# The low part of q on all 128 partitions: the second score pass of a differential attention at 128 rows

## Chip, cores, metric

One core of a Trainium2 chip runs the whole program. The metric is device time in microseconds of one execution. The engines are TensorE (PE in the profile; its weight loads appear as a lane of their own, PEld), VectorE (DVE), ScalarE (ACT), GpSimd (POOL) and SyncE (SP), which issues most DMAs.

## What is computed

Two layers of a hybrid decoder on a sequence of 512 tokens, width 1024. In each layer one input projection feeds four mixers (an S5 state space, a differential attention, an RG-LRU and a cross-attention into 256 memory tokens), each is gated, and an output projection is added to x. The change lies in the differential attention, of which this is the core of the reference:

```python
s1 = jnp.einsum('bqhd,bkhd->bhqk', qblk[..., 0, :], k1).astype(F32)
s2 = jnp.einsum('bqhd,bkhd->bhqk', qblk[..., 1, :], k2).astype(F32)
s1 = jnp.where(mask, s1, -1e30)
s2 = jnp.where(mask, s2, -1e30)
p = jax.nn.softmax(s1, axis=-1) - lam * jax.nn.softmax(s2, axis=-1)
return jnp.einsum('bhqk,bkhd->bqhd', p.astype(v.dtype), v)
```

There are 4 heads with two 64-wide halves m = 0, 1 each, a causal mask, and query blocks of 128.

## The kernel before

Everything is f32. To use the faster f32r matmuls without losing precision, the kernel splits an operand into a high part (rounded to f32r by a cast) and a low part (what the cast left over), and multiplies high by high, high by low and low by high, accumulating in PSUM. The projections (`cm_block`, matmul line L508, and `tm_block`, matmul line L528) do that with three passes per piece of weight, 128 rows by 256 or 512 columns, and they make up most of TensorE's work. ScalarE casts the weights' high part (`whi`, L166), VectorE subtracts the low part (`wlo`, L172).

Attention (`attention`, L601) runs beside these projections as a generator: after each piece of a projection a tick lets the live generators put in their next step, and the Tile scheduler then fixes the order on each engine and gives out the buffers of the pools. Items are pairs (query block i, head h), 16 per layer. `scores(n)` makes, for m = 0 and 1, a tile of scores of N = 128 (i + 1) columns, but at least 256 are streamed. The keys `kT[m]` hold on the 64 partitions of half m the high part of k and on the other 64 partitions its low part. The queries' high part `qh` stands on both halves of the partitions, so that one pass with 128 rows (L638) gives qh·k_high + qh·k_low. The second pass (L639) multiplies the queries' low part `ql` by k_high: it uses only the 64 partitions of half m, both of the stationary tile and of the keys. A third pass (L640), in bf16, adds the causal mask from an identity and a constant tile. There are 64 of each pass in the program. Then VectorE takes the maximum (L642), ScalarE the exponentials into `e` (L648), VectorE combines both halves (L654); later TensorE transposes (`ptrans`, L662) and multiplies by v (`av`, L672).

`q_parts(i)` is called at the first head of a block: two casts per half on ScalarE (L622, L623) fill both partition halves of `qh`, and one subtraction per half on VectorE (issued in the helper `tt`, L340) fills `ql`. `qh` comes from the pool `mid` (tag b4, four buffers of 4 KB per partition), which also holds `e`, the memory tiles and the normalised x; `ql` comes from `sm2` (tag b2, nine buffers of 2 KB).

Of the kernel before, what the change touches and what calls it, by code (L numbers as in the profile page):

```python
# [10 lines left out]
F32R = mybir.dt.float32r  # L11
# [3 lines left out]
ALU = mybir.AluOpType  # L15
AX = mybir.AxisListType

P = 128
# [72 lines left out]
def tile_kernel(ctx: ExitStack, tc: tile.TileContext, A, out):  # L91
    nc = tc.nc
    V, S, G, PE = nc.vector, nc.scalar, nc.gpsimd, nc.tensor
# [11 lines left out]
    def nm(s):  # L105
        uid[0] += 1
        return f"{s}_{uid[0]}"
# [4 lines left out]
    def b4(shape, name, dtype=F32):  # L112
        return mid.tile(shape, dtype, tag="b4", name=nm(name))

    def b2(shape, name, dtype=F32):
        return sm2.tile(shape, dtype, tag="b2", name=nm(name))

    def ti(n, name):
        return tiny.tile([P, n], F32, tag=name, name=nm(name))
# [4 lines left out]
    def sc2(shape):  # L124
        return ps.tile(list(shape), F32, tag="sc", bufs=1, name=nm("sc"))

    def tp(shape=(P, 4, 128)):
        return ps.tile(list(shape), F32, tag="tp", bufs=2, name=nm("tp"))

    def ms(shape):  # L130
        return ps.tile(list(shape), F32, tag="tp", bufs=2, name=nm("ms"))
# [153 lines left out]
    def norm_h(t):  # L285

        h = b4([P, D], "h")
        r = rstd_of(xs(t), D, h)
        scale_h(h, t, r)
        return h  # L290
# [27 lines left out]
    for t in range(NT):  # L318
        h, hn = hn, (norm_h(t + 1) if t + 1 < NT else None)
# [19 lines left out]
    def tt(o, a, b, op):  # L339
        V.tensor_tensor(out=o, in0=a, in1=b, op=op)  # L340
# [260 lines left out]
    def attention(l, R):  # L601
        while pend or "par" in st.live:
            yield
        qT, kT, v = R["qT"][0], R["kT"], R["v"]
        o = qT
        R["o"] = o
        oss = const.tile([P, 16], F32, tag="oss", name=nm("oss"))
        R["oss"] = oss
        items = [(i, h) for i in range(NT) for h in range(4)]
        n_it = len(items)  # L610
        live = {}

        qs_ = {}

        def q_parts(i):

            qi = qT[:, :, i * 128:(i + 1) * 128]
            qh = b4([P, 2, 4, 128], "qh", F32R)
            ql = b2([P, 4, 128], "ql", F32R)
            for m in range(2):  # L620
                own, oth = slice(m * 64, m * 64 + 64), slice(64 - m * 64, 128 - m * 64)
                S.copy(qh[own, m], qi[own])  # L622
                S.copy(qh[oth, m], qi[own])  # L623
                tt(ql[own], qi[own], qh[own, m], ALU.subtract)
            qs_[i] = (qh, ql)

        def scores(n):
            i, h = items[n]
            N = (i + 1) * 128

            M = max(N, 256)
            s = sc2((P, 2, 512))
            if h == 0:
                q_parts(i)
            qh, ql = qs_[i]
            for m in range(2):
                own = slice(m * 64, m * 64 + 64)
                PE.matmul(s[:, m, :M], qh[:, m, h, :], kT[m][:, h, :M], start=True, stop=False)  # L638
                PE.matmul(s[:, m, :M], ql[own, h, :], kT[m][own, h, :M], start=False, stop=False)  # L639
                PE.matmul(s[:, m, i * 128:N], idb, cmb, start=False, stop=True)  # L640
            mx = ti(2, "mx")
            V.tensor_reduce(out=mx, in_=s[:, :, :N], op=ALU.max, axis=AX.X)  # L642
            nmx = ti(2, "nmx")
            V.tensor_scalar(out=nmx, in0=mx, scalar1=-0.125, scalar2=None, op0=ALU.mult)
            e = b4([P, 2, 512], "e")
            sm = ti(2, "sm")
            for m in range(2):
                S.activation(e[:, m, :N], s[:, m, :N], AF.Exp, bias=nmx[:, m:m + 1], scale=0.125,  # L648
                             accum_out=sm[:, m:m + 1])
            rc = ti(2, "rc")  # L650
            V.reciprocal(rc, sm)
            cc = ti(1, "cc")
            V.tensor_scalar(out=cc, in0=sm[:, 0:1], scalar1=nlam[:, l:l + 1], scalar2=rc[:, 1:2], op0=ALU.mult, op1=ALU.mult)
            V.scalar_tensor_tensor(out=e[:, 0, :N], in0=e[:, 1, :N], scalar=cc, in1=e[:, 0, :N], op0=ALU.mult, op1=ALU.add)  # L654
            live[n] = (e, rc, None)

        def ptrans(n):
            i, h = items[n]
            e, rc, _ = live[n]
            pt = tp()  # L660
            for j in range(i + 1):
                PE.transpose(pt[:, j, :], e[:, 0, j * 128:(j + 1) * 128], ident)  # L662
            pT = b2([P, 4, 128], "pT")
            S.copy(pT[:, :i + 1, :], pt[:, :i + 1, :])
            live[n] = (None, rc, pT)

        def av(n):
            i, h = items[n]
            _, rc, pT = live.pop(n)
            a = ms((P, 128))  # L670
            for j in range(i + 1):
                PE.matmul(a, pT[:, j, :], v[:, j, h * 128:(h + 1) * 128], start=(j == 0), stop=(j == i))  # L672
            S.activation(o[:, h, i * 128:(i + 1) * 128], a, AF.Copy, scale=rc[:, 0:1])
            jk = b2([P, 128], "jk")
            S.activation(jk, a, AF.Square, scale=rc[:, 0:1], accum_out=oss[:, i * 4 + h:i * 4 + h + 1])

        for n in range(n_it + 2):
            if n < n_it:
                scores(n)
            if n >= 2:  # L680
                av(n - 2)
            yield D_AT[0]
            if 1 <= n <= n_it:
                ptrans(n - 1)
                yield D_AT[1]
# [416 lines left out]
    for pi, (l, n, u, ids) in enumerate(plan):  # L1102
# [93 lines left out]
        elif n == "gl":  # L1196
# [4 lines left out]
            for hf, pid in enumerate(ids):  # L1201
                whi, wlo = (w.rearrange("p (k s c) -> p k s c", k=2, s=2) for w in w_use(pid))
                for j in range(2):
                    for s in (1, 0):
                        a = gacc[j][s]
                        i = 0
                        for k in range(2):
                            for w, h in ((whi, yhi), (whi, ylo), (wlo, yhi)):
                                PE.matmul(a, w[:, k, s, j * 128:(j + 1) * 128], h[:, 2 * hf + k, :],  # L1209
                                          start=(hf == 0 and i == 0), stop=(hf == 1 and i == 5))  # L1210
# [112 lines left out]
```

## Time and profile before

| | |
|---|---|
| median of 3 runs | 934.51 us (934.37 to 934.92) |
| profiled execution | 934.99 us |
| its span, first to last instruction | 933.2 us |
| mean granted TensorE clock | 0.997 |
| busy: PE, PEld, DVE, ACT, POOL | 908.3, 751.0, 645.2, 521.4, 42.8 us |

A row of the timeline gives the start of an instruction in us from the start of the span, its length, engine, line and operands. Matmuls are pipelined, so their lengths overlap: what a matmul costs is the distance from its start to the next one's, and the length holds the way through the array as well. The windows give busy time by engine in a stretch; the chain follows the work that ended last back from release to release.

### The profile page before, as it was taken

How to read it: one execution, taken by the hardware profiler on the slowest of the kernel's cores; microseconds unless marked ns; L12 is line 12 of the kernel's file. 1: busy time of each engine (PE TensorE's matmuls, PEld its weight loads, DVE VectorE, ACT ScalarE, POOL GpSimd, SP SyncE). 2: the span in 40 equal slices, each digit the busy share in tenths (PEclk: the TensorE clock that was granted, in tenths of full speed). 3: DMA queues.
4: the chain of work that ended last, by engine and by line, in shares of the span. 5: the costliest groups of instructions: out<-in, count | busy, mean ns of one | idle time of the engine just before them, and what ended most of it. 6: DMA issues, size and time to landing. Idle time of an engine off the chain costs nothing.

```text
span 933.2 us, 12492 instructions
## 1 busy us (share of the span) xinstructions
PE 908.3 (97%) x4538; PEld 751.0 (80%) x4538; DVE 645.2 (69%) x1297; ACT 521.4 (56%) x1038; POOL 42.8 (5%) x94
## 2 busy tenths in 40 slices
PE   6999999999999989999999999999999999999997
PEld 4788878877888878888888888788778888788885
DVE  6975877458999965893373675853698998667343
ACT  6674776987343355831454579665646333764123
POOL 1001000001011100000100000000101110000000
PEclk9999999999999999999999999999999999999999
DMA  5833432103213225532343321421212222243222
GB/s 198 210 103 99 137 91 68 46 23 94 68 50 116 71 69 186 142 113 91 106 162 105 91 91 46 147 89 59 72 48 70 72 72 68 68 155 117 93 88 91
DMA packets 81072, 90.59 MB, mean 97 GB/s; under 512 B 23793, under 2 KB 58226, under 8 KB 81010
## 3 DMA queue, kind: packets, MB, share of 16 engines
q1 hardware_dynamic: 77986, 85.98, 29.8%
q10 hardware_dynamic: 720, 2.62, 0.8%
q0 software_dynamic: 2304, 1.18, 0.5%
q8 instruction: 36, 0.59, 0.3%
q14 instruction: 26, 0.21, 0.1%
HBM read 84.92 MB, written 4.19 MB: 95 GB/s over the span
## 4 chain that ended last, share of the span: by engine, by line
PE 78%; DVE 14%; ACT 4%; DMA 2%; issue 2%; SPq 1%; DVEq 0%; ACTq 0%
PE acc L528 37%; PE acc L508 19%; PE acc L1209 5%; DVE u L340 3%; PE sc L639 2%; DVE wlo L172 2%; PE ms L672 2%; PE tp L1032 1%; PE sc L638 1%; DVE xr L1015 1%; PE sc L640 1%; PE tp L826 1%; PE tp L305 1%; PE tp L662 1%; PE sc L801 1%
## 5 line engine op out<-in xcount | busy, mean ns | idle before, releaser
L166 ACT CAST whi<-raw 128x1024 fp32r<-128x1024 f32 x136 | 143.2, 1053 | 224.4 <-PE acc L528 123.8
L172 DVE TENSOR_TENSOR wlo<-raw,whi 128x1024 fp32r<-128x1024 f32 x136 | 166.1, 1222 | 120.8 <-ACT whi L166 120.3
L508 PE MATMUL acc<-hThi,whi 128*128 128x512 f32 x384 | 155.3, 404 | 0.3 <-DVE bg L709 0.3
L508 PE MATMUL acc<-hThi,wlo 128*128 128x512 f32 x384 | 153.1, 399 | 0.0
L508 PE MATMUL acc<-hTlo,whi 128*128 128x512 f32 x384 | 152.7, 398 | 0.0
L528 PE MATMUL acc<-whi,hThi 128*128 128x512 f32 x256 | 105.1, 410 | 0.8 <-ACT whi L166 0.8
L528 PE MATMUL acc<-wlo,hThi 128*128 128x512 f32 x256 | 101.7, 397 | 0.0
L528 PE MATMUL acc<-whi,hTlo 128*128 128x512 f32 x256 | 101.1, 396 | 0.0
L528 PE MATMUL acc<-whi,mxl 128*128 128x512 f32 x256 | 100.2, 391 | 0.0
L528 PE MATMUL acc<-whi,mxh 128*128 128x512 f32 x256 | 100.2, 391 | 0.0
L528 PE MATMUL acc<-wlo,mxh 128*128 128x512 f32 x256 | 100.2, 391 | 0.0
L508 PEld LDWEIGHTS acc<-hThi,wlo 128*128 128x128 f32 x384 | 72.6, 189 | 14.2
L508 PEld LDWEIGHTS acc<-hThi,whi 128*128 128x128 f32 x384 | 72.7, 189 | 13.5 <-DVE bg L709 0.7
L508 PEld LDWEIGHTS acc<-hTlo,whi 128*128 128x128 f32 x384 | 72.8, 190 | 12.9
L528 PEld LDWEIGHTS acc<-whi,hThi 128*128 128x128 f32 x256 | 56.4, 220 | 8.9 <-ACT whi L166 1.2
L528 PEld LDWEIGHTS acc<-whi,hTlo 128*128 128x128 f32 x256 | 56.3, 220 | 7.7 <-DVE hTlo L308 0.2
L528 PEld LDWEIGHTS acc<-wlo,hThi 128*128 128x128 f32 x256 | 56.6, 221 | 7.1
L528 PEld LDWEIGHTS acc<-whi,mxl 128*128 128x128 f32 x256 | 48.1, 188 | 9.8
L528 PEld LDWEIGHTS acc<-whi,mxh 128*128 128x128 f32 x256 | 48.1, 188 | 9.7
L528 PEld LDWEIGHTS acc<-wlo,mxh 128*128 128x128 f32 x256 | 48.1, 188 | 9.6
L642 DVE TENSOR_REDUCE mx<-sc 128x2 f32<-128x256 f32 (+3 forms) x32 | 26.3, 823 | 36.3 <-PE sc L640 36.2
L966 POOL DMA_DIRECT2D MT<-kq x64 | 32.1, 508 | 376.3 <-DVE kq L340 233.5
(305 smaller groups left out, 1671.5 us busy)
## 6 DMA issues: line engine op xcount, KB each, us to landing
raw<-in_w_in_dram SPq DMA_DIRECT2D x80, 512.0 KB, 3.6
raw<-in_w_out_dram SPq DMA_DIRECT2D x32, 512.0 KB, 3.3
raw<-in_w_mem_kv_dram SPq DMA_DIRECT2D x16, 512.0 KB, 3.3
x<-in_x_dram SPq DMA_DIRECT2D x8, 512.0 KB, 5.2
raw<-in_s_w_glu_dram SPq DMA_DIRECT2D x16, 256.0 KB, 3.1
mt<-in_mem_dram SPq DMA_DIRECT2D x4, 512.0 KB
xd<-x SPq DMA_DIRECT2D x4, 512.0 KB, 4.3
x<-xd SPq DMA_DIRECT2D x4, 512.0 KB, 7.0
```

What stands on the lines that cost most here:

```text
L166: S.copy(hi, wbuf[j])
L172: V.tensor_tensor(out=lo, in0=raw, in1=hi, op=ALU.subtract)
L305: lastins["pe"] = PE.transpose(pt[:, k, :], h[:, kk * 128:(kk + 1) * 128], ident)
L340: V.tensor_tensor(out=o, in0=a, in1=b, op=op)
L508: PE.matmul(a[j][:, :ncol], w[:, kk, c], h(k), start=(hf == 0 and i == 0), stop=(hf == 1 and i == 3 * nh - 1))
L528: PE.matmul(a[t], h(k, t), w[:, kk, :], start=(p == 0 and kk == 0 and i == 0), stop=(p == np_ - 1 and kk == 1 and i == 2))
L638: PE.matmul(s[:, m, :M], qh[:, m, h, :], kT[m][:, h, :M], start=True, stop=False)
L639: PE.matmul(s[:, m, :M], ql[own, h, :], kT[m][own, h, :M], start=False, stop=False)
L642: V.tensor_reduce(out=mx, in_=s[:, :, :N], op=ALU.max, axis=AX.X)
L672: PE.matmul(a, pT[:, j, :], v[:, j, h * 128:(h + 1) * 128], start=(j == 0), stop=(j == i))
L966: G.dma_start(out=MT[g * 64 + 64 - n:g * 64 + 64, g, t], in_=kq[g * 64:g * 64 + n])
L1209: PE.matmul(a, w[:, k, s, j * 128:(j + 1) * 128], h[:, 2 * hf + k, :], start=(hf == 0 and i == 0), stop=(hf == 1 and i == 5))
```

## The change

`ql` gets the shape of `qh`, one copy per half m, from the pool `mid`. For each half the subtraction is made twice, once onto the half's own partitions and once, from the same inputs, onto the other 64. The second pass then takes all 128 rows of `ql` and of `kT[m]`: besides ql·k_high it adds ql·k_low, a term that was left out before.

```diff
             qh = b4([P, 2, 4, 128], "qh", F32R)
-            ql = b2([P, 4, 128], "ql", F32R)
+            ql = b4([P, 2, 4, 128], "ql", F32R)
             for m in range(2):
                 own, oth = slice(m * 64, m * 64 + 64), slice(64 - m * 64, 128 - m * 64)
                 S.copy(qh[own, m], qi[own])
                 S.copy(qh[oth, m], qi[own])
-                tt(ql[own], qi[own], qh[own, m], ALU.subtract)
+                tt(ql[own, m], qi[own], qh[own, m], ALU.subtract)
+                tt(ql[oth, m], qi[own], qh[own, m], ALU.subtract)
...
             for m in range(2):
-                own = slice(m * 64, m * 64 + 64)
                 PE.matmul(s[:, m, :M], qh[:, m, h, :], kT[m][:, h, :M], start=True, stop=False)
-                PE.matmul(s[:, m, :M], ql[own, h, :], kT[m][own, h, :M], start=False, stop=False)
+                PE.matmul(s[:, m, :M], ql[:, m, h, :], kT[m][:, h, :M], start=False, stop=False)
                 PE.matmul(s[:, m, i * 128:N], idb, cmb, start=False, stop=True)
```

The scheduler orders the engines anew. On TensorE, at the first item of layer 0's third query block (`sc` is the tile of scores, `acc` a projection's accumulator), the order before was:

```order
L638 MATMUL sc_1599<-kT_751,qh_1600 128x384
L639 MATMUL sc_1599<-kT_751,ql_1601 128x384
L640 LDWEIGHTS idb
L640 MATMUL sc_1599<-cmb,idb 128x128
L672 MATMUL ms_1627<-v_546,pT_1578 128x128
L638 MATMUL sc_1599<-kT_752,qh_1600 128x384
L672 MATMUL ms_1627<-v_546,pT_1578 128x128
L508 MATMUL acc_1633<-hThi_122,whi_1489 128x512
L639 MATMUL sc_1599<-kT_752,ql_1601 128x384
```

and of the change, from the last of the dense matmuls that now stand between the first and the second pass:

```order
L508 MATMUL acc_1639<-hThi_122,wlo_1495 128x512
L639 MATMUL sc_1603<-kT_751,ql_1605 128x384
L640 LDWEIGHTS idb
L640 MATMUL sc_1603<-cmb,idb 128x128
L638 MATMUL sc_1603<-kT_752,qh_1604 128x384
L662 MATMUL tp_1659<-cst,e_1539 128x128 x2
```

Twelve projection matmuls now stand between the item's first L638 and its L639, and eight between the second L638 and its L639, where there was one.

On VectorE, at the last query block of layer 1 (`rc`, `cc`, `e`: the softmax of the item before; `mx`: the maximum of the new one), the order before was:

```order
L654 SCALAR_TENSOR_TENSOR e_6087<-e_6087,cc_6093 128x384
L340 TENSOR_TENSOR ql_6157<-qT_4578,qh_6156 64x512 x2
L172 TENSOR_TENSOR wlo_6200<-raw_6037,whi_6198 128x1024
L642 TENSOR_REDUCE mx_6170<-sc_6155 128x2
L340 TENSOR_TENSOR qm_6030<-acc_6031,qm_6029 128x512
```

and of the change:

```order
L654 SCALAR_TENSOR_TENSOR e_6101<-e_6101,cc_6107 128x384
L340 TENSOR_TENSOR ql_6171<-qT_4586,qh_6170 64x512 x4
L172 TENSOR_TENSOR wlo_6216<-raw_6051,whi_6214 128x1024
L642 TENSOR_REDUCE mx_6186<-sc_6169 128x2
L340 TENSOR_TENSOR qm_6044<-acc_6045,qm_6043 128x512
```

The place is the same, with four subtractions in it instead of two.

## Rows read from the trace of the kernel before

**Rows 1.** The page, busy time and share of the span by engine.
```profile
PE 908.3 (97%) x4538; PEld 751.0 (80%) x4538; DVE 645.2 (69%) x1297; ACT 521.4 (56%) x1038; POOL 42.8 (5%) x94
```

**Rows 2.** The chain that ended last, shares by line.
```profile
by line: PE acc L528 37.1%; PE acc L508 18.6%; PE acc L1209 4.6%; DVE u L340 3.1%; PE sc L639 2.4%; DVE wlo L172 1.9%; PE ms L672 1.8%; issue 1.5%; PE tp L1032 1.4%; PE sc L638 1.4%; DVE xr L1015 1.4%; PE sc L640 1.1%; PE tp L826 1.1%; PE t
```

**Rows 3.** Windows: stretch, its length, busy PE, PEld, DVE, ACT, POOL, PEclk, DMA.
```profile
85.00:210.00 125.00, 124.88 (x638) 101.39 (x637) 82.28 (x159) 96.87 (x212) 3.93 (x10) 1.00 0.24 74
577.00:693.00 116.00, 116.00 (x603) 94.67 (x601) 77.81 (x152) 68.42 (x167) 4.04 (x8) 1.00 0.26 78
655.00:700.00 45.00, 45.00 (x231) 34.63 (x230) 37.12 (x73) 22.99 (x54) 4.04 (x8) 1.00 0.18 53
700.00:800.00 100.00, 98.70 (x551) 84.26 (x550) 88.32 (x161) 47.60 (x107) 12.00 (x24) 1.00 0.23 71
```

**Rows 4.** Waits of the weight loads: who waited for whom, total us, times, longest.
```profile
PEld sc L639 <- issue: 10.0, 38, 0.4
...
PEld L640 <- issue: 6.6, 31, 0.2
...
PEld sc L639 <- DVE ql L340: 0.4, 1, 0.4
```

**Rows 5.** Timeline of the weight loads around one item of 256 columns.
```profile
101.94 0.19 PEld L638 LDWEIGHTS sc<-kT,qh 128*128 128x128 f32 x1
102.26 0.18 PEld L639 LDWEIGHTS sc<-kT,ql 64*128 64x128 f32 x1
102.57 0.10 PEld L640 LDWEIGHTS <-idb 128*128 128x128 bf16 x1
102.58 0.20 PEld L638 LDWEIGHTS sc<-kT,qh 128*128 128x128 f32 x1
```

**Rows 6.** Timeline of the matmuls around the same item.
```profile
101.93 0.28 PE L508 MATMUL acc<-mhi,wlo 128*128 128x256 f32 x1
102.05 0.28 PE L638 MATMUL sc<-kT,qh 128*128 128x256 f32 x1
...
103.26 0.37 PE L508 MATMUL acc<-mhi,whi 128*128 128x256 f32 x1
103.46 0.27 PE L662 MATMUL tp<-cst,e 128*128 128x128 f32 x1
```

**Rows 7.** Matmuls, an item of 384 columns: its first, and the one behind it.
```profile
632.00 0.34 PE L638 MATMUL sc<-kT,qh 128*128 128x384 f32 x1
...
633.47 0.33 PE L672 MATMUL ms<-v,pT 128*128 128x128 f32 x1
```

**Rows 8.** Matmuls, an item of 512 columns, with the dense matmul ahead of it.
```profile
657.33 0.39 PE L508 MATMUL acc<-hThi,wlo 128*128 128x512 f32 x1
657.56 0.39 PE L638 MATMUL sc<-kT,qh 128*128 128x512 f32 x1
...
658.76 0.49 PE L639 MATMUL sc<-kT,ql 64*128 64x512 f32 x1
...
659.25 0.55 PE L672 MATMUL ms<-v,pT 128*128 128x128 f32 x3
```

**Rows 9.** The chain in order of time: 14 matmuls of 128 columns in a row.
```profile
708.82 1.56 PE sc L986 x14
```

**Rows 10.** Tile ql, its subtractions: ns least/median/most, first and last start.
```profile
L340 DVE TENSOR_TENSOR ql<-qT,qh x16: 673/684/689, 89.4 to 657.1; 64x512 fp32r<-64x512 f32 x16
```

**Rows 11.** Timeline of VectorE at the last query block of layer 1.
```profile
654.88 0.68 DVE L340 TENSOR_TENSOR ql<-qT,qh 64x512 fp32r<-64x512 f32 x1
657.09 0.69 DVE L340 TENSOR_TENSOR ql<-qT,qh 64x512 fp32r<-64x512 f32 x1 [1.53 <-ACT qh L622]
```

**Rows 12.** Timeline, layer 1: transposes of e, an exponential, a block's last scores.
```profile
636.91 0.49 PE L662 MATMUL tp<-cst,e 128*128 128x128 f32 x3
...
644.11 0.58 ACT L648 ACTIVATE e<-sc,nmx 128x384 f32<-128x384 f32 x1 [0.77 <-DVE nmx L644]
...
649.32 0.42 PE L638 MATMUL sc<-kT,qh 128*128 128x384 f32 x1
```

## The prediction

> **What bounds the kernel now.** I read the totals of the page first. TensorE is busy 97% of the span [rows 1], and three of its lines make 60% of the chain that ended last; the three lines of the scores (L638, L639, L640) hold 4.9% of that chain, some 46 us [rows 2]. Then the stretches in which attention runs, layer 0 from 85 to 210 us and layer 1 from 577 to 693 us: TensorE has work without a gap in both (124.88 of 125 us, 116 of 116), at a granted clock of 1.00, the 2.4 GHz level, while VectorE is busy 66 and 67% [rows 3]. So what TensorE spends on a score item is on the path, as long as nobody else becomes late.
>
> Next the waits of the weight loads. The load of the 64-row pass (L639) stands idle for 10.0 us in 38 cases, and the load behind it (L640) for 6.6 us in 31, and neither waits for a semaphore that the profile shows [rows 4]. These count only idle time of the load path; what they cost TensorE shows in the timeline of one item. In the dense stream before it the load of the next stationary tile begins 0.01 us after the running matmul (load L638 at 101.94, matmul L508 at 101.93) and a matmul starts every 0.12 us. But the load of L639 comes only at 102.26, 0.21 us after the matmul L638 at 102.05, so it waited until that matmul had nearly streamed; and the load of L640 comes 0.31 us after L639. The next load of L638 begins 0.01 us after that of L640: no hold between those two, though one is bf16 and the other f32 [rows 5, 6]. What holds loads, then, goes with the change from 128 rows to 64 and back. That is the reading on which the forecast rests.
>
> **The change part by part.** (1) L639 becomes a 128-row pass. It streams the same columns, so nothing is added on TensorE; the two holds around it (128 to 64, 64 to 128) should go, 128 per kernel. One item of 256 columns now lasts from 102.05 to 103.26, and the matmul behind it starts its successor after 0.20 instead of 0.12 us: 1.29 us [rows 6]. Without holds I charge four f32 passes at the dense spacing of 0.12, and two bf16 passes at the 0.11 us that 14 matmuls of 128 columns take each (1.56 us / 14) [rows 9]: 0.70 us, so 0.59 saved. For 384 columns the item lasts 632.00 to 633.47, 1.47 us [rows 7]; four passes at 0.175 (an estimate between 0.12 for 256 and 0.23 for 512) and 0.22 make 0.92: 0.55 saved. For 512 columns 657.56 to 659.25, 1.69 us, against 4 x 0.23 + 0.22 = 1.14: 0.55 again [rows 8]. Over two layers there are 16 items of 256, 8 of 384 and 8 of 512 columns: 16 x 0.59 + 16 x 0.55 = 18.2 us. If the 0.08 us behind an item counts for the longer ones too, it is 19.5.
>
> Here the Trainium skill speaks against the change. TensorE: Matmul & The Clock Gate, Part 3 ("Packing small matmuls"), says that a weight load overlaps a running matmul only where their row groups differ. By it the 128-row load would still be held and the 18.2 us would be nothing. The trace disagrees: 128-row loads run under 128-row matmuls all through the dense stream [rows 5, 6], and it is the load with other rows that is held.
>
> (2) Two more subtractions per block of queries on VectorE, 16 in all at 0.684 us, 10.9 us [rows 10]. In the attention stretches they raise its busy time by 5.5 us each, to some 88 of 116 us and 83 of 107: covered as work, by TensorE's dense projections. As latency they stand between the casts and the scores. At the last block of layer 1 the two subtractions ended at 655.56 and 657.78 [rows 11]; with two more the second pair ends at 657.09 + 2 x 0.69 = 658.47. The second 64-row pass stood at 658.76; without holds it is due at 657.56 + 0.23 + 0.23 + 0.11 + 0.23 = 658.36 [rows 8], so TensorE would wait 0.1 us. If no slack is left, a boundary costs the whole lag of the second pair, 0.78 us. Six boundaries have this (the first block of each layer is prepared ahead): 0.6 to 4.7 us. Before, TensorE waited 0.4 us for this tile in the whole kernel [rows 4], and the order now puts other matmuls ahead of the second pass in layer 0's third block, so I stay near the lower end: 1.6 us. Without that cover it is 4.7.
>
> (3) The tile moves to a ring of four buffers that it shares with qh, the exponentials e and others. Two stay for e. An exponential at 644.11 needs the buffer that was last read by the transposes at 636.91, 6.7 us earlier; and the next block's subtraction at 654.88 came over 5 us after the last block's scores at 649.32 [rows 11, 12]. I cost this at nothing; the cover is that distance.
>
> (4) In layer 1 the last block runs beside the S5 part. From 655 to 800 us VectorE is busy 125.4 of 145 us [rows 3]. Four items save 2.2 us there and two added subtractions cost VectorE 1.4. Between nothing lost and all of it (3.6), I take 2.4, because TensorE too is nearly gapless there, 143.7 of 145. In layer 0 attention ends before its S5 part begins, which then simply starts earlier.
>
> (5) The scheduler orders everything anew. The passes' counts are the same and I find no stall in the new rows: nothing, with 1 us either way.
>
> Sum, against the profiled execution of 934.99 us (span 933.2 and 1.8 around it): 934.99 - 18.2 + 1.6 + 2.4 = 920.8. That execution stands 0.5 us above the median of the runs, 934.51, so I forecast **920.3 us**.
>
> **The rivals.**
> *The bf16 mask pass still waits.* No row shows f32 followed by bf16 at equal rows, only the reverse. If the kind of number holds the load, half of the holds stay: 64 x 0.09 us (0.21 against 0.12) = 5.8 us less saved, 926.1. For it: L640 is held today. Against it: bf16 to f32 is not held [rows 5].
>
> *VectorE becomes the bound in layer 1.* If TensorE then waits for maxima and S5 products from 577 us on, layer 1's 9.1 us are lost and 1.4 us of subtractions are added; with 0.8 us at layer 0's boundaries: 934.99 - 9.1 + 1.4 + 0.8 = 928.1, 927.6 as a median. For it: 88.3 of 100 us busy from 700 to 800. Against it: 67% in the stretch itself [rows 3]. It decides where VectorE has more than about nine tenths to do in the shortened stretch.
>
> *The hold remains and the subtractions are bare: slower.* If a load of q's low part is held for some reason other than its rows, nothing is saved on TensorE, and 1.6 us at boundaries and 1.4 us in the S5 stretch are added: 938.0, a median of 937.5. It decides as soon as the load of L639 still comes 0.2 us after the matmul of L638. Against it: 128-row loads in the dense stream are not held. The rule of the Trainium skill cited above (TensorE: Matmul & The Clock Gate, Part 3) would end here.
>
> *The change does nothing.* The same hold, but the subtractions lie under the dense matmuls: 934.5.
>
> **How the numbers follow.** Forecast 0.59, own range 915 to 923; mask pass held 0.17; VectorE bound 0.12; nothing 0.06; slower 0.06. The low end is 19.5 us saved and no cost, 934.5 - 19.5 = 915.0. The high end takes in the first two rivals, the second with 1.5 us more at the boundaries: 929.0. The two cases left out hold 0.12, and some of the forecast's tail lies outside too. A difference under 0.2%, 1.9 us, can hardly be told from none here: faster 0.88, same 0.06, slower 0.06.
>
> **What would show it.** Right: the load of L639 starts about 0.01 us after the matmul of L638; L638, L639 and L640 follow at 0.12, 0.12 and 0.11 us for 256 columns; the idle rows of L639 and L640 vanish; both attention stretches get shorter by about 9 us; ql counts 32 subtractions. Wrong in part: L640's load still comes 0.2 us behind L639 (mask pass), or TensorE shows new waits for ql, the maxima or S5 tiles (VectorE). Wrong outright: L639's own load still 0.2 us late.

## The result, and the profile after

The changed kernel takes 924.08 us (median of 4 runs, 923.76 to 924.45), before 934.50 (4 runs, 934.37 to 934.92): a ratio of 0.9888, 95% interval 0.9872 to 0.9904, 10.4 us faster. The forecast was 920.3 with a range of 915.0 to 929.0, so sign and range held and the gain was 3.8 us smaller than forecast (14.2). The profiled execution took 923.84 us, its span is 922.1 at a mean granted clock of 0.997, as before.

The page of the changed kernel, busy time by engine, answers to [rows 1]; under it the chain that ended last by line, for [rows 2], and the subtractions' row, for [rows 10]:

```profile
PE 894.3 (97%) x4538; PEld 748.3 (81%) x4538; DVE 655.7 (71%) x1313; ACT 519.1 (56%) x1036; POOL 42.9 (5%) x94
```
```profile
by line: PE acc L528 35.7%; PE acc L508 14.8%; PE acc L1209 4.7%; DVE u L340 4.0%; DVE wlo L172 3.0%; issue 1.8%; PE tp L1032 1.7%; DVE xr L1015 1.7%; PE ms L672 1.3%; PE tp L826 1.3%; PE sc L638 1.2%; ACT whi L166 1.1%; PE tp L305 1.0%; PE
```
```profile
L340 DVE TENSOR_TENSOR ql<-qT,qh x32: 662/686/691, 56.3 to 647.3; 64x512 fp32r<-64x512 f32 x32
```

The second pass held 2.4% of the chain and the mask 1.1%; now neither is above 1.0%. TensorE lost 14.0 us of busy time, more than the kernel gained; VectorE got 10.5 us more, sixteen subtractions of 0.686 us. What VectorE's lines hold of the chain has grown (`wlo` from 1.9 to 3.0%, `u` from 3.1 to 4.0%).

One item of 256 columns in layer 1, first the matmuls, then the weight loads; compare [rows 5, 6]:

```profile
571.23 0.28 PE L508 MATMUL acc<-mhi,wlo 128*128 128x256 f32 x1
571.35 0.28 PE L638 MATMUL sc<-kT,qh 128*128 128x256 f32 x1
571.47 0.28 PE L639 MATMUL sc<-kT,ql 128*128 128x256 f32 x1
571.59 0.23 PE L640 MATMUL sc<-cmb,idb 128*128 128x128 bf16 x1
571.63 0.36 PE L638 MATMUL sc<-kT,qh 128*128 128x256 f32 x1
571.83 0.28 PE L639 MATMUL sc<-kT,ql 128*128 128x256 f32 x1
571.95 0.23 PE L640 MATMUL sc<-cmb,idb 128*128 128x128 bf16 x1
571.99 0.36 PE L508 MATMUL acc<-mhi,whi 128*128 128x256 f32 x1
572.19 0.28 PE L508 MATMUL acc<-mlo,whi 128*128 128x256 f32 x1
```
```profile
571.35 0.19 PEld L639 LDWEIGHTS sc<-kT,ql 128*128 128x128 f32 x1
571.59 0.10 PEld L640 LDWEIGHTS <-idb 128*128 128x128 bf16 x1
571.59 0.20 PEld L638 LDWEIGHTS sc<-kT,qh 128*128 128x128 f32 x1
```

The load of L639 now starts with the matmul L638 (both at 571.35), where it came 0.21 us later. From 571.35 to 571.99 the item lasts 0.64 us, and the matmul behind it starts its successor after 0.20 instead of 0.12: 0.72 in all, against 1.29 before and 0.70 charged. The load of the bf16 mask is the odd one: it comes 0.12 us after the matmul L639 has started, when that has streamed, not under it. But the mask's own matmul then holds the next one up by 0.04 only, and the pass after that is 0.08 late: 0.12 in all, against 0.11 charged.

Waits of the weight loads, in the columns of [rows 4]:

```profile
PEld L640 <- issue: 6.3, 29, 0.3
...
PEld sc L638 <- ACT e L648: 2.8, 9, 0.5
...
PEld sc L639 <- DVE ql L340: 1.7, 4, 0.6
PEld tp L699 <- ACT th L708: 1.5, 1, 1.5
...
PEld tp L662 <- DVE e L654: 0.9, 1, 0.9
```

L639's 10.0 us without a releaser are gone. L640's row stays, 6.3 us in 29 cases, for the reason just seen: the load path is idle there, and TensorE is not. New or longer are waits for others: the exponentials (2.8 us; 1.3 before), `ql` (1.7; 0.4 before), and tanh of the RG-LRU (`th`, 1.5, not before).

The windows, for [rows 3]:

```profile
85.00:210.00 125.00, 124.36 (x674) 105.33 (x673) 92.98 (x175) 104.09 (x226) 3.99 (x10) 1.00 0.27 83
577.00:693.00 116.00, 114.81 (x633) 97.50 (x631) 86.81 (x170) 70.89 (x183) 4.04 (x8) 1.00 0.28 88
```
```profile
700.00:800.00 100.00, 97.30 (x526) 81.35 (x525) 84.72 (x152) 49.47 (x103) 8.00 (x16) 1.00 0.21 65
```

The same stretches hold 36 and 30 matmuls more. TensorE had gaps of 0.1 and 0.0 us there before and has 0.6 and 1.2 now. If the distances between starts of successive matmuls are added up over the whole kernel, less the dense spacing of each size (0.11, 0.12, 0.175 and 0.23 us for 128, 256, 384 and 512 columns), the excess is 43.7 us before and 32.6 after; in front of L639 and L640 it fell from 21.3 to 4.7. So **16.5 us went at the holds and about 5 came back at other lines.** Before, a hold was 0.14 us on average in front of L639 and 0.19 in front of L640.

Where, shows the first matmul of the S5 part's last projection (L1209; first and last start in the row) in both layers; before, and under it now:

```profile
L1209 PE MATMUL acc<-yhi,whi x64: 388/390/477, 348.2 to 837.2; 128*128 128x512 f32 x64
```
```profile
L1209 PE MATMUL acc<-yhi,whi x64: 389/389/478, 342.1 to 826.0; 128*128 128x512 f32 x64
```

Layer 0 gave 6.1 us and layer 1 another 5.1; the forecast had 9.1 of savings in each, before its charges.

### The profile page after: what moved, and what is told of

It reads as the page before. It is cut to its first block, busy times and chain, and to the rows that moved or that the text cites. A ratio compares the mean times of both kernels' runs of the same rounds, so it can differ in the third digit from the quotient of the medians.

```text
span 922.1 us, 12510 instructions
## 1 busy us (share of the span) xinstructions
PE 894.3 (97%) x4538; PEld 748.3 (81%) x4538; DVE 655.7 (71%) x1313; ACT 519.1 (56%) x1036; POOL 42.9 (5%) x94
## 4 chain that ended last, share of the span: by engine, by line
PE 70%; DVE 18%; ACT 6%; DMA 3%; issue 2%; SPq 1%; DVEq 0%; ACTq 0%
PE acc L528 36%; PE acc L508 15%; PE acc L1209 5%; DVE u L340 4%; DVE wlo L172 3%; PE tp L1032 2%; DVE xr L1015 2%; PE ms L672 1%; PE tp L826 1%; PE sc L638 1%; ACT whi L166 1%; PE tp L305 1%; PE sc L639 1%; DVE VV L340 1%; PE sc L801 1%
## 5 line engine op out<-in xcount | busy, mean ns | idle before, releaser
L508 PE MATMUL acc<-hThi,whi 128*128 128x512 f32 x384 | 155.0, 404 | 0.0
L508 PE MATMUL acc<-hThi,wlo 128*128 128x512 f32 x384 | 152.8, 398 | 0.0
L508 PE MATMUL acc<-hTlo,whi 128*128 128x512 f32 x384 | 152.2, 396 | 0.0
L528 PE MATMUL acc<-whi,hThi 128*128 128x512 f32 x256 | 105.9, 414 | 0.8 <-ACT whi L166 0.8
L528 PE MATMUL acc<-wlo,hThi 128*128 128x512 f32 x256 | 101.3, 396 | 0.0
L528 PE MATMUL acc<-whi,hTlo 128*128 128x512 f32 x256 | 101.0, 395 | 0.0
L528 PE MATMUL acc<-whi,mxh 128*128 128x512 f32 x256 | 100.1, 391 | 0.0
L528 PE MATMUL acc<-whi,mxl 128*128 128x512 f32 x256 | 100.1, 391 | 0.0
L528 PE MATMUL acc<-wlo,mxh 128*128 128x512 f32 x256 | 100.1, 391 | 0.0
L508 PEld LDWEIGHTS acc<-hThi,wlo 128*128 128x128 f32 x384 | 72.7, 189 | 14.3
L508 PEld LDWEIGHTS acc<-hThi,whi 128*128 128x128 f32 x384 | 72.7, 189 | 12.9
L508 PEld LDWEIGHTS acc<-hTlo,whi 128*128 128x128 f32 x384 | 72.7, 189 | 12.9
L528 PEld LDWEIGHTS acc<-whi,hThi 128*128 128x128 f32 x256 | 56.3, 220 | 8.9 <-ACT whi L166 1.2
L528 PEld LDWEIGHTS acc<-whi,hTlo 128*128 128x128 f32 x256 | 56.1, 219 | 7.9 <-DVE hTlo L308 0.2
L528 PEld LDWEIGHTS acc<-wlo,hThi 128*128 128x128 f32 x256 | 56.7, 221 | 7.1
L528 PEld LDWEIGHTS acc<-whi,mxh 128*128 128x128 f32 x256 | 48.1, 188 | 9.8
L528 PEld LDWEIGHTS acc<-whi,mxl 128*128 128x128 f32 x256 | 48.1, 188 | 9.8
L528 PEld LDWEIGHTS acc<-wlo,mxh 128*128 128x128 f32 x256 | 48.1, 188 | 9.6
L648 ACT ACTIVATE e<-sc,nmx 128x128 f32<-128x128 f32 (+3 forms) x64 | 33.3, 530 | 11.7 <-DVE nmx L644 10.2
```

What stands on the lines that cost most here:

```text
L508: PE.matmul(a[j][:, :ncol], w[:, kk, c], h(k), start=(hf == 0 and i == 0), stop=(hf == 1 and i == 3 * nh - 1))
L528: PE.matmul(a[t], h(k, t), w[:, kk, :], start=(p == 0 and kk == 0 and i == 0), stop=(p == np_ - 1 and kk == 1 and i == 2))
```

## The experiments

The theory after the result: 128 rows take the holds away, and three things bear on what comes out: the saving itself, the sixteen subtractions, and the new home of `ql` in the ring of four buffers, with the order that the scheduler makes of it. The rivals put the 3.8 us on one of these alone. The runs before on the same chips had medians of 934.6 to 934.9.

**The doubled subtractions and the new tile, with 64 rows.** Of the change, only the second pass is undone.

```diff
-                PE.matmul(s[:, m, :M], ql[:, m, h, :], kT[m][:, h, :M], start=False, stop=False)
+                own = slice(m * 64, m * 64 + 64)
+                PE.matmul(s[:, m, :M], ql[own, m, h, :], kT[m][own, h, :M], start=False, stop=False)
```

> The changed kernel's tile (in the ring of four) and its doubled subtractions, but the second pass still takes 64 rows: it leaves the added term ql.k_low out, as the kernel before did. So TensorE gains nothing, and the run shows what the rest of the change costs by itself. If the 7 us that the changed kernel gave back are the price of the subtractions or of the ring: 939 to 942 us. If they are neither, but waits that only a faster TensorE uncovers: 934 to 936 us. In both cases the loads of L639 stay 0.21 us behind the matmul of L638.

Measured 943.82 us (941.36 to 944.32), ratio 1.0088 (1.0075 to 1.0102): 9 us slower than before. So the preparations, with the order that comes with them, cost more than either reading gave them, and the rows must have brought more than 10.4 us.

**The ring alone.** The kernel before, with `ql` taken from the pool of `qh` and `e` and nothing else.

```diff
-            ql = b2([P, 4, 128], "ql", F32R)
+            ql = b4([P, 4, 128], "ql", F32R)
```

> The kernel before with nothing changed but the place of ql: the ring of four buffers (its shape, its two subtractions and the 64 rows stay). If the ring is what gave time back: 939 to 941 us. If it was the subtractions, or waits that a faster TensorE uncovers: 934 to 936 us.

Measured 943.22 us (941.11 to 944.2), ratio 1.0088 (1.0074 to 1.0101). One word costs 8.5 us. The 0.6 that the subtractions add on top of it is no difference: the single runs of the two kernels cover the same times. If the traces are lined up row by row, 64 of VectorE's 1297 rows and 214 of TensorE's 4538 stand outside the longest order that this kernel and the one before share, though the work is the same.

The place where most is lost is the end of attention in layer 0. TensorE in this kernel, from the transposes of one item to the scores of the next, with the releaser in brackets:

```profile
192.75 0.49 PE L662 MATMUL tp<-cst,e 128*128 128x128 f32 x3
193.81 0.94 PE L672 MATMUL ms<-v,pT 128*128 128x128 f32 x6 [0.57 <-ACT pT L664]
194.58 0.60 PE L662 MATMUL tp<-cst,e 128*128 128x128 f32 x4
197.18 0.79 PE L638 MATMUL sc<-kT,qh 128*128 128x512 f32 x1 [2.00 <-ACT e L648]
197.90 0.79 PE L639 MATMUL sc<-kT,ql 64*128 64x512 f32 x1
```

and ScalarE at the same time:

```profile
193.28 0.48 ACT L664 COPY pT<-tp 128x384 f32<-128x384 f32 x1 [0.93 <-PE tp L662]
193.65 0.72 ACT L739 ACTIVATE li<-lr,cpos 128x512 f32<-128x512 f32 x1
194.38 1.28 ACT L648 ACT_TABLE_LOAD   x1
195.68 0.69 ACT L648 ACTIVATE e<-sc,nmx 128x512 f32<-128x512 f32 x1
```

In the kernel before, twelve dense matmuls of L508 stood between the same transposes (192.97) and the L672 behind them (196.05), and the exponentials were ready in time. In the new order L508 comes later: of its matmuls 192 have run when these scores begin, 211 before. Between the scores of the item ahead and these stand 14 dense matmuls of L508 and L528, 25 before. On ScalarE the exponentials have moved behind the copy of `pT` (193.28), which came after the first of them before. `sc` has one buffer, so the next scores wait until the exponentials have read it: TensorE waits 2.00 us for exponentials that stand behind a switch of ScalarE's function table. The Trainium skill (ScalarE activation tables: per-element evaluation and per-set limits, "What a function is on this engine") gives 1283 ns for such a load; the row agrees with 1.28. With the wait TensorE falls to half its rate. Windows of this kernel, columns as in [rows 3]:

```profile
195.00:197.00 2.00, 0.18 (x2) 0.00 (x0) 0.00 (x0) 1.99 (x5) 0.00 (x0) 0.92 0.75 248
197.00:199.00 2.00, 1.82 (x4) 0.89 (x4) 1.09 (x3) 2.00 (x8) 0.00 (x0) 0.50 0.00 0
199.00:201.00 2.00, 2.00 (x5) 1.09 (x5) 1.27 (x3) 2.00 (x5) 0.00 (x0) 0.50 0.00 0
201.00:203.00 2.00, 2.00 (x7) 1.62 (x7) 1.42 (x3) 1.85 (x5) 0.00 (x0) 0.50 0.00 0
```

The granted clock is 0.50, the 1.2 GHz level, and the matmul L638 of 512 columns takes 0.72 us to its successor instead of 0.23 (dense) or 0.32 (with a hold). In these four windows it costs up to 2 x (0.08 + 3 x 0.50) = 3.2 us, with the wait up to 5 of the 8.5. Not every execution falls so: of the four runs three show a mean clock of 0.992 to 0.995 and took 942.79 to 944.20 us, and one shows 0.997, as the kernel before in its profiled execution, and took 941.11.

**128 rows in this order, without added subtractions.** The change, with the other half of `ql` set to zero by GpSimd instead.

```diff
-                tt(ql[oth, m], qi[own], qh[own, m], ALU.subtract)
+                G.memset(ql[oth, m].bitcast(F32), 0.0)
```

> The changed kernel with 128 rows and the ring, but the other half of ql is filled with zeros by GpSimd instead of by a second subtraction (so the term ql.k_low is left out, as before). VectorE does the 16 subtractions of the kernel before. If the doubled subtractions gave the time back: 917 to 920 us. If it was the ring or uncovered waits: 923 to 925 us.

Measured 926.03 us (925.77 to 926.36), ratio 0.9907 (0.9893 to 0.992). On TensorE, VectorE and ScalarE the order of this kernel is, row for row, that of the ring alone, so 128 rows instead of 64 are the difference: 943.22 - 926.03 = 17.2 us. And it is 1.95 us *slower* than the full change: sixteen more subtractions, and the order that comes with them, took less time. At the place just read that order has 24 dense matmuls where the ring alone has 14, and no wait of 2.00 us.

**A fifth buffer.** The change with five buffers in the ring; to make room, `sm2` has eight instead of nine and four small tables share one tile.

```diff
-    mid = ctx.enter_context(tc.tile_pool(name="mid", bufs=4))
-    sm2 = ctx.enter_context(tc.tile_pool(name="sm2", bufs=9))
+    mid = ctx.enter_context(tc.tile_pool(name="mid", bufs=5))
+    sm2 = ctx.enter_context(tc.tile_pool(name="sm2", bufs=8))
```

> The changed kernel with five buffers in the ring instead of four; to make room the other pool has eight instead of nine, and four small parameter tiles lie in a table that is not in use yet. If the ring gave the time back: 917 to 920 us. If it was the subtractions or uncovered waits: 923 to 925 us.

Measured 930.2 us (929.85 to 931.35), ratio 0.9955 (0.9942 to 0.9967): 6.1 us slower than the change. Neither figure came; a tight ring alone would have got better. But 221 rows of VectorE leave the order of before (78 in the change) and `sm2` is smaller, so it tells only that more buffers in the ring, with that order, don't bring back the loss.

**The rows alone, at the old order.** The kernel before with one line changed: the second pass takes all 128 partitions of `ql` as it stands.

```diff
-                own = slice(m * 64, m * 64 + 64)
+                own = slice(0, P)
```

> The kernel before with one edit: the second pass takes all 128 partitions of ql as it is, so that the rows of the other half add that half's low part times the low part of this half's k, a product of two low parts that does not belong to the scores, instead of nothing. No added subtraction, no new buffer, and on each engine all but some rows stand in the order of the kernel before. If the holds of the weight loads were worth what the prediction charged and the rest of the change gave time back: 916 to 919 us. If a faster TensorE uncovers waits by itself: 922 to 925 us, as the changed kernel. If the hold had another cause than the rows: 934 to 935 us.

Measured 919.62 us (919.22 to 919.96), ratio 0.9838 (0.9823 to 0.9853). Only 2 rows of VectorE, 4 of ScalarE and 26 of TensorE's 4538 leave the order of before. So the rows bring 15.3 us where the order all but stays, 0.6 above the range given for the charged holds, and all that the change adds around them costs 924.08 - 919.62 = 4.5 us. Its waits, in the columns of [rows 4]:

```profile
PEld L640 <- issue: 6.6, 31, 0.3
...
PEld sc L638 <- ACT e L648: 2.0, 6, 0.4
```

The difference of 15.3 to the 17.2 above lies in the granted clock. Layer 0 has a pause in every kernel, where TensorE waits for VectorE's `wt` before L948: 1.21 us before, 1.20 with the rows alone.

```profile
225.80 0.63 PE L948 MATMUL tp<-cst,wt 128*128 128x128 f32 x4 [1.21 <-DVE wt L340]
```
```profile
218.21 0.63 PE L948 MATMUL tp<-cst,wt 128*128 128x128 f32 x4 [1.20 <-DVE wt L340]
```

Windows of 2 us behind it, before:

```profile
226.00:228.00 2.00, 2.00 (x15) 1.81 (x14) 2.00 (x3) 1.96 (x5) 0.00 (x0) 0.83 0.00 0
228.00:230.00 2.00, 2.00 (x6) 1.52 (x5) 1.94 (x6) 1.93 (x5) 1.69 (x4) 0.50 0.39 108
230.00:232.00 2.00, 2.00 (x13) 1.81 (x12) 1.96 (x5) 0.43 (x1) 2.00 (x5) 0.82 0.59 186
```

and with the rows alone:

```profile
218.00:220.00 2.00, 1.79 (x14) 1.77 (x15) 2.00 (x3) 1.97 (x3) 0.00 (x0) 1.00 0.00 0
220.00:222.00 2.00, 2.00 (x11) 1.65 (x10) 1.94 (x6) 1.92 (x7) 1.26 (x3) 1.00 0.22 37
222.00:224.00 2.00, 2.00 (x18) 1.92 (x17) 1.96 (x5) 0.85 (x1) 2.00 (x5) 1.00 0.76 251
```

The same pause is followed by a fall to 0.50 in the one and by none in the other. The fall costs up to 2 x (0.17 + 0.50 + 0.18) = 1.7 us, but less of it arrives: from this L948 to L1044, where TensorE waits for the S5 part, the traces take 109.2 us before and 108.5 with the rows alone. Nor does it belong to the kernel. Of the 25 runs of the kernel before that stand beside the experiments, five show a mean clock of 0.997, as the profiled one, and took 935.15 us on average; twenty show 0.998 or 0.999 and took 934.63. So such a fall is worth some 0.5 us here.

Leaving out the last 20 us of the program, where TensorE runs out of work in all of them, the profiled executions of before, the change and the 128 rows with the ring have one such fall each; that of the rows alone has none; that of the ring alone has the long one above and another at 230 us, together three windows of 5 us at 0.67, 0.65 and 0.66, up to 5 x (0.33 + 0.35 + 0.34) = 5.1 us. So runs at the same clock have to be compared. At the old order, without a fall, they average 934.63 before and 919.61 with the rows alone: 15.0 us. In the ring's order, with a mean clock of 0.997, one run took 941.11 at 64 rows and three average 925.95 at 128: 15.2. The two orders agree within 0.2 us, though the second hangs on one run; the doubled subtractions with 64 rows, too, have one run at 0.997, of 941.36 us. By the same runs the ring with its order costs 941.11 - 935.15 = 6.0 us at 64 rows and 925.95 - 919.61 = 6.3 at 128, of which some 0.5 is a fall that only the first of the two has.

**The 64-row passes grouped.** The kernel before; of an item, first both passes L638, then both L639, then both masks.

```diff
-            for m in range(2):
-                own = slice(m * 64, m * 64 + 64)
-                PE.matmul(s[:, m, :M], qh[:, m, h, :], kT[m][:, h, :M], start=True, stop=False)
-                PE.matmul(s[:, m, :M], ql[own, h, :], kT[m][own, h, :M], start=False, stop=False)
-                PE.matmul(s[:, m, i * 128:N], idb, cmb, start=False, stop=True)
+            own = [slice(0, 64), slice(64, 128)]
+            for p, m in ((0, 0), (0, 1), (1, 0), (1, 1), (2, 0), (2, 1)):
+                if p == 0: PE.matmul(s[:, m, :M], qh[:, m, h, :], kT[m][:, h, :M], start=True, stop=False)
+                if p == 1: PE.matmul(s[:, m, :M], ql[own[m], h, :], kT[m][own[m], h, :M], start=False, stop=False)
+                if p == 2: PE.matmul(s[:, m, i * 128:N], idb, cmb, start=False, stop=True)
```

> The kernel before with 64 rows, its passes put in another order within an item: both first passes, both second passes, both mask passes. The rows change twice in an item instead of four times, and the two second passes use different halves of the rows. If a hold goes with each change between 128 and 64 rows, half of them are saved, 8 to 9 us less: 925 to 927 us if the load for the other half is free of the pass that runs, 928 to 931 us if it too is held. If the 64-row pass is slow by itself, however it is placed: 934 to 936 us.

Measured 922.05 us (921.62 to 922.52), ratio 0.9864 (0.985 to 0.9879): better than expected, and better than the change. TensorE at an item of 384 columns:

```profile
622.85 0.51 PE L638 MATMUL sc<-kT,qh 128*128 128x384 f32 x2
623.29 0.44 PE L639 MATMUL sc<-kT,ql 64*128 64x384 f32 x2
623.66 0.28 PE L640 MATMUL sc<-cmb,idb 128*128 128x128 bf16 x2
```

The two second passes, one on partitions 0 to 63 and one on 64 to 127, take 0.37 us together from 623.29 to 623.66, the hold behind them included. They run at the same time: both lie in a length of 0.44, which one such pass has by itself in the kernel before,

```profile
632.27 0.44 PE L639 MATMUL sc<-kT,ql 64*128 64x384 f32 x1
```

and in the trace the second starts 0.003 us behind the first, in every size; the two loads start as close together, so the load for the other half isn't held. In that the Trainium skill (TensorE: Matmul & The Clock Gate, Part 3) is right: it says that matmuls on different parts of the array overlap. From the first of the two to the mask it is 0.32 us at 256 columns, 0.38 at 384 and 0.44 at 512 (medians), against 0.24, 0.35 and 0.46 for two 128-row passes in the grouped kernel further down.

**Two small tiles instead of the ring.** The change with `ql` as two tiles of the old pool.

```diff
-            ql = b4([P, 2, 4, 128], "ql", F32R)
+            ql = [b2([P, 4, 128], "ql", F32R) for _ in range(2)]
```

> The changed kernel (128 rows, doubled subtractions) with the low part in two tiles from the pool it came from instead of one tile from the ring of four. If the ring is what gave time back: 916 to 919 us. If the subtractions are: 923 to 926 us. If it is the order that the scheduler comes to, whatever moved it: neither figure is bound to come, and waits of TensorE at other places than in the changed kernel.

Measured 925.9 us (924.7 to 926.58), ratio 0.9905 (0.9889 to 0.9922): not faster than the change. The old pool doesn't bring the 4.5 us back. The time lies in the range given for the subtractions, but the sign of the third reading is there too: TensorE waits at new places, 1.21 us at L672 (107.96) among them, and 89 rows each of VectorE and ScalarE leave the order of before. With the fifth buffer this speaks against the ring as a store of too few buffers; what the costly kernels share is that the order moved.

**The rows alone, grouped.** Both together: `own` is `slice(0, P)` and the passes stand in the order of the grouped kernel.

```diff
-            own = [slice(0, 64), slice(64, 128)]
+            own = [slice(0, P), slice(0, P)]
```

> Rows_alone with the passes of an item grouped: both first passes, both second passes, both mask passes, all of 128 rows (the second pass again adds a product of two low parts that does not belong to the scores). In the trace a pass behind a mask pass starts its successor 0.08 us late; grouping leaves one such place in an item instead of two. 32 x 0.08 = 2.6 us less than rows_alone: 917 us. If grouped_64 was quicker than expected because passes side by side are cheaper whatever their rows, and not because two halves of the rows ran at the same time: 913 to 915 us.

Measured 918.46 us (917.93 to 918.97), ratio 0.9825 (0.9811 to 0.9838), the lowest time in the study. Against the rows alone the intervals overlap, so nothing is claimed for the grouping at 128 rows. The 913 to 915 us for passes that are cheaper side by side whatever their rows didn't come, so the gain of the grouped 64-row passes is their running at the same time and the holds saved.

**The subtractions by themselves.** The rows alone with each subtraction made twice, in place.

```diff
-                tt(ql[own], qi[own], qh[own, m], ALU.subtract)
+                for _ in range(2): tt(ql[own], qi[own], qh[own, m], ALU.subtract)
```

> Rows_alone with each of its 16 subtractions done twice into the same place: the work on VectorE that the change adds (10.9 us), without a new tile. If the subtractions cost what the prediction charged, or a little: 920 to 922 us. If they cost nothing and the order, which shifts a little, stays as good: 919 to 920 us. If a shifted order is what costs: 922 to 926 us, with waits of TensorE at new places.

Measured 923.08 us (922.45 to 924.07), ratio 0.9876 (0.9863 to 0.989): 3.5 us more than the rows alone. The clock falls to 0.81 and 0.85 between 220 and 230 us, behind the pause at L948, but that explains little: the run without a fall (0.999) took 922.45, and the like run of the rows alone 919.22. 38 rows of VectorE and 49 of ScalarE left the order of before, and TensorE has a new wait of 0.96 us for exponentials at L638 (107.50), the sign of a shifted order; so this isn't the price of the sixteen instructions alone either. Against three partners the same sixteen gave +0.6 (no difference by the runs' spread), -1.9 and +3.5 us: whatever price of their own they have, an order change of this size hides it.

## Why the prediction was right, and where it was off

**Term 1, the holds (18.2 us): right in its mechanism, too large.** The load of L639 comes with the matmul L638, as forecast, and an item of 256 columns takes 0.72 us against 0.70 charged. The rule of the Trainium skill that spoke against it (TensorE: Matmul & The Clock Gate, Part 3: a load overlaps a running matmul only where the row groups differ) would, taken by itself, have left nothing of it; the trace of the change disagrees, with a 128-row load starting at 571.35 together with a 128-row matmul. At the holds 16.5 us went, 0.52 for each of the 32 items on average where one item of each size had given 0.59 and 0.55; in the time of the kernel 15.0 to 15.2 at the same clock, in two orders. Part of the rest turned into waits for others, for which the term had nothing: with the rows alone loads of L638 wait 2.0 us for the exponentials, 1.3 before.

**Term 2, the subtractions (+1.6): right where they stand.** The waits of L639's loads for `ql` rose from 0.4 to 1.7 us, 1.3 more. As a change to the whole kernel no price of their own could be found (above). The 0.78 us for a boundary without slack has no row behind it; the rows give 658.47 - 657.78 = 0.69, so that the upper end is 4.1 and not 4.7.

**Terms 3 and 5, the ring at nothing and the scheduler's order at nothing "with 1 us either way": these failed.** Rows moved on every engine for a tile of 2 KB in another pool, and the price was 8.5 us at 64 rows and 6.4 at 128 (926.03 - 919.62), about 6 in both at the same clock. I had shown that buffers come free in time, and took that for a proof that nothing happens. At the place that was read the cost is not a wait for a buffer of the ring, since ScalarE goes into the table switch without a pause (193.65 + 0.72 against 194.38); it is dense matmuls that no longer stand under the exponentials: 2.00 us at L638 in the kernels with the ring alone, at 64 and at 128 rows, and in some runs a fall of the clock with it. The full change escaped that one place, with 24 dense matmuls there instead of 14: its longest wait for the exponentials is 0.5 us. Which link of the ring's order is the decisive one, the buffer or the priorities that the scheduler derives, stays open: no run holds the order fixed while the pool changes.

**Term 4, layer 1 beside S5 (+2.4): the amount came, by luck; the reason did not show.** Layer 1 gave 5.1 of its 9.1 us with the change and 6.8 with the rows alone, where L1209 begins and ends so:

```profile
L1209 PE MATMUL acc<-yhi,whi x64: 389/389/477, 339.9 to 822.1; 128*128 128x512 f32 x64
```

That is 2.3 lost, as charged. But from layer 1's first scores to its last L672 the time fell by 7.1 us (131.0 to 123.9), and from there to L1209, beside S5, it rose by 0.4, with TensorE's wait for VectorE's `mpT` at L826 now 1.0 instead of 0.6. So 2.0 of the 2.3 were lost in attention itself, and so was 1.0 in layer 0, which has no S5 part beside it (134.0 to 125.9 from the first scores to L948, 8.1 of 9.1). That belongs to term 1. In the full change the stretch behind attention holds the new wait at L699, which no run sets apart from the order.

**The sum.** Forecast 18.2 - 4.0 = 14.2. Measured 15.3 for the rows, where terms 1 and 4 together had 15.8, less 4.5 for order and subtractions together (the ring +6.4, the rest of the change -1.9), where terms 2, 3 and 5 had 1.6: 10.8, and 0.4 of it is the difference between two chips' runs of before. Of the miss of 3.8 us 2.9 is the reorder, with the subtractions, which couldn't be told from it. That the time stayed within the range is owed to its width: the 1 us that term 5 allowed for the order would not have covered it.

**The rivals.** *The mask pass still waits*: half right. The mask's load still waits until L639 has streamed (0.24 us behind L639's load, the sign I had named), but the price of 5.8 us didn't come, since the pass costs the 0.12 us that it was charged with 0.11 for. *VectorE bound in layer 1* (927.6): refuted as a whole, since the stretch from 577 to 693 us kept TensorE busy for 114.81 of 116; the new waits in layer 1 for `e` and `th`, 1.5 us and less each, may be its small form. *Hold remains* and *nothing*: refuted by the first load.

## What to carry to other kernels

Here a weight load for 64 rows behind a 128-row matmul, and one for 128 rows behind a 64-row matmul, was held until that matmul had nearly streamed, while the loads of 128 rows behind 128 and of one half of the rows behind the other were not. A pass over half the rows in a stream of full ones can so cost more than the full pass; where the unused rows hold something harmless, taking all rows is free on TensorE, and where they don't, two passes over the two halves side by side saved nearly as much (12.8 us). In a kernel whose order a scheduler makes, price every edit that touches pools, tile shapes or instruction counts with the few us that a new order brings, of either sign, and look for the variant that leaves the order alone: here one changed line gave 15.3 us, at the price of a small product that doesn't belong to the scores, and the full edit 10.4. To know what a part is worth, compare two kernels of the same order, and runs at the same granted clock.

## What the runs showed of the hardware that was not expected

Two 64-row passes on different halves of the partitions, one straight behind the other, ran at the same time: 0.37 us for both at 384 columns, and at 512 the pair was quicker (0.44) than two 128-row passes (0.46). The same pause of 1.20 to 1.21 us on TensorE was followed by a fall of the granted clock to 0.50 in one trace and by none in another; runs of one and the same kernel differ so too, by some 0.5 us in the kernel before and by 1.7 to 3.1 us with the ring alone. A bf16 load behind an f32 pass of the same rows comes 0.12 us late in a stream of 256 columns and still costs the next passes no more than 0.12 us together.
